# Gated linear attention: three buffers for values by chunk and states, and a step's features requested one step early

## The chip, the cores and the metric

The kernel runs on one core of a Trainium2 chip. The metric is the time of one execution on the device in microseconds (us). A plain time is the median of several timed executions; the profile is one further execution, recorded by the hardware profiler.

The core has a matmul engine (PE), a vector engine (DVE), a scalar engine (ACT), a general engine (POOL), and a queue engine (SP) that issues most DMA loads. ACT issues most stores. Each engine takes its instructions in its own order.

## The reference, cut to what matters

One layer of a hybrid token mixer on x of 2048 tokens by 1024 features: an adaptive normalisation, one projection to 13 groups of columns, three mixers (gated linear attention "GLA", a second gated linear attention "HGRN", and stick-breaking attention), gates, an output projection, a residual and a last normalisation. The stage that the change touches computes this twice, for GLA (4 heads, 64 key and 128 value features each) and for HGRN (4 heads, 64 and 64):

```python
def step(state, inp):                       # one chunk of 64 tokens
    q_c, k_c, v_c, g_c = inp
    b_cum = jnp.cumsum(g_c, axis=2)
    diff = b_cum[:, :, :, None, :] - b_cum[:, :, None, :, :]
    decay = jnp.exp(jnp.where(causal, diff, -jnp.inf))
    scores = jnp.einsum('bhtd,bhsd,bhtsd->bhts', q_c, k_c, decay)
    o_c = (jnp.einsum('bhts,bhsv->bhtv', scores, v_c)
           + jnp.einsum('bhtd,bhdv->bhtv', q_c * jnp.exp(b_cum), state))
    b_last = b_cum[:, :, -1:, :]
    state = (jnp.exp(b_last[:, :, 0, :, None]) * state
             + jnp.einsum('bhsd,bhsv->bhdv', k_c * jnp.exp(b_last - b_cum), v_c))
    return state, o_c
```

## The kernel before

The program first makes all projections and writes them to DRAM, then computes the stick-breaking attention mixed with further projections, then the linear-attention stage, and last the output stage (phase2).

The linear-attention stage has 16 steps. A step is one pair of heads and 512 tokens (8 chunks of 64): steps 0 to 7 are GLA (two pairs, four steps each), steps 8 to 15 are HGRN. In this stage PE's order is written by hand (`manual_schedule(engines={ENG.PE})`). The order on SP, ACT, DVE and POOL is made by the framework's planner when the program is built: it places an instruction by its planned readiness (inputs there, buffer free), and among ready ones by their place in the text. A tile with `bufs=2` has two buffers in turn; a new tile waits until the last reader of the tile that held its buffer is done.

A step runs as follows.

- Loads on SP: three features bc, qt, kt (128x512, 256 KB each, lines 897 to 899, three buffers each); the values once by blocks, Vn (line 823, two buffers; 512 KB in GLA, 256 KB in HGRN), and once by chunks, Vv, in two halves (line 835, two buffers; 256 KB a half in GLA, 128 KB in HGRN). Vn feeds U, Vv feeds o.
- ACT, DVE and POOL: exponentials eP (907), and of bc (910) or kt (915); products (911, 912, 916); kd (917, on POOL, written over kt in GLA and over bc in HGRN); Qd (918, three buffers).
- PE: scp (924), the scores; four transposes ptk of kd (848). ACT copies scp to S (928) and ptk to KTt (850).
- PE: 9 fill matmuls of a gate projection (269); U = KTt x Vn (858); 9 more fill matmuls; then o of the step before (880), which reads Vv, Ms, St and Qd; ACT copies it to oe (884) and stores it.
- DVE: eight state updates (867), one for each chunk, `St[n+1] = St[n] * decay + U[n]`; the last one writes the first state of the next step's tile, Sn. St has two buffers. The last step of a pair has seven updates. At the first step of a pair POOL clears the first state (831).

The order written for PE, with `i` the step:

```python
for i, tail in enumerate(gla_fast(GLA_ORDER, gp, gr_, pp, scp)):   # scp of step i
    next(tail)                  # ptk of step i
    run(fill, GLA_F[0])
    next(tail)                  # U and state updates of step i
    ...
    if i >= 8:
        with tc.issue_after(om[0].ins):
            next(ws, None)      # scale_wo: one more part of the output weights
    run(fill, GLA_F[1])
    if before is not None:
        run(before, 1)          # o of step i - 1
    before = tail
```

`om[0]` is the last state update issued; the parts of `scale_wo` (load wr, line 1019; product on POOL, 1020; wh and wl on DVE, 1023 and 1024) are placed behind it on their engines as far as it is theirs, which is DVE. The raw weights wr share two buffers (tag `wraw`) with the raw gate weights wraw (load 149, whi on ACT 150, wlo on DVE 151).

Of the kernel before, what the change touches and what calls it, by code (L numbers as in the profile page):

```python
# [8 lines left out]
F32 = mybir.dt.float32  # L9
# [3 lines left out]
AF = mybir.ActivationFunctionType  # L13
ALU = mybir.AluOpType
# [4 lines left out]
P = 128  # L19
T = 2048  # L20
# [4 lines left out]
CB = 64  # L25
GTF = 512
ORDER = (3, 2, 1, 0)
NBF = GTF // CB
# [14 lines left out]
def hybrid_mixer_kernel(ctx, tc, x, c, w_ada, b_ada, w_in, w2, bg, gnw, lbl, hnw,  # L43
                        w_out, fnw, masks, sel2, out):
    nc = tc.nc
    mm = nc.tensor.matmul
# [13 lines left out]
    class Chunks:  # L60
# [4 lines left out]
        def __getitem__(self, at):  # L65
# [4 lines left out]
    s_feat = {n: [Chunks(f"s_{n}{j}") for j in range(2)]  # L70
              for n in ("qa", "ka", "z", "qb", "fb", "da", "db", "kb")}
# [15 lines left out]
    def rms_scale(ss):  # L87
# [10 lines left out]
                            compare_op=ALU.is_gt, fill=0.0)  # L98
# [5 lines left out]
    SE = const.tile([P, 4, T // GTF, 3 * NBF], F32, name="SE")  # L104
# [119 lines left out]
    ld, ha, dv = [None], [None], [None]  # L224
# [68 lines left out]
    with tc.manual_schedule(engines={ENG.PE, ENG.DVE, ENG.Activation, ENG.Pool}):  # L293
# [132 lines left out]
        tiles = [x1, load_x(ORDER[2], p0x), None]  # L426
# [37 lines left out]
        for i in (1, 2):  # L464
            n = ORDER[i]
# [8 lines left out]
    n = ORDER[3]  # L474
# [30 lines left out]
    with tc.issue_after(ha[0].ins), tc.issue_after(dv[0].ins):  # L505
# [12 lines left out]
        loml = const.tile([P, 2], F32, name="loml")  # L518
# [10 lines left out]
    def v3(ap, t=CB):  # L529
        return ap.rearrange("p (n t) -> p n t", t=t)  # L530
# [282 lines left out]
    hpools[ORDER[2]].close()  # L813


    def load_values(pools, pr, g, GT, Sn):
        gla = pr < 2
        j = pr % 2
        dv = 128 if gla else 64
        NB = GT // CB  # L820
        vcols = (s_va if gla else s_ib)[g * GT:(g + 1) * GT, j * 2 * dv:(j + 1) * 2 * dv]
        Vn = pools.tile([P, GT // P, 2 * dv], F32, tag="Vn", name="Vn")
        nc.sync.dma_start(Vn, vcols.rearrange("(b p) d -> p b d", p=P))


        def new_s():
            return pools.tile([P, NB, dv], F32, tag="St", name="St", bufs=2)
        St = Sn
        if St is None:
            St = new_s()  # L830
            nc.gpsimd.memset(St[:, 0, :], 0.0)
        Vv = pools.tile([P, NB, dv], F32, tag="Vv", name="Vv", bufs=2)
        vr = vcols.rearrange("(n p) d -> p n d", p=CB)
        for h in range(2):
            nc.sync.dma_start(Vv[h * 64:(h + 1) * 64], vr[:, :, h * dv:(h + 1) * dv])
        return Vn, Vv, St, new_s() if g + 1 < T // GT else None
# [3 lines left out]
    def gla_tail(gr_, pp, pr, g, GT, Ms, Qd, kd, dec, Vn, Vv, St, Sn):  # L840
        gla = pr < 2
        j = pr % 2
        dv = 128 if gla else 64
        NB = GT // CB

        ptk = pp.tile([P, GT // P, P], F32, tag="ptk", name="ptk")
        for b in range(GT // P):
            nc.tensor.transpose(ptk[:, b, :], kd[:, b * P:(b + 1) * P], ident)
        KTt = gr_.tile([P, GT // P, P], F32, tag="KTt", name="KTt")
        nc.scalar.copy(KTt, ptk)  # L850
        yield


        U = [pp.tile([P, NB // 2, dv], F32, tag=f"U{e}", name=f"U{e}") for e in range(2)]
        for n in range(NB):
            rs = slice((n % 2) * 64, (n % 2) * 64 + 64)
            for h in range(2):
                mm(U[n % 2][h * 64:(h + 1) * 64, n // 2, :], KTt[rs, n // 2, h * 64:(h + 1) * 64],
                   Vn[rs, n // 2, h * dv:(h + 1) * dv], start=True, stop=True)
        for n in range(NB):  # L860
            if n + 1 < NB:
                dst = St[:, n + 1, :]
            elif Sn is not None:
                dst = Sn[:, 0, :]
            else:
                continue
            om[0] = nc.vector.scalar_tensor_tensor(dst, St[:, n, :], dec[:, n:n + 1], U[n % 2][:, n // 2, :],
                                           op0=ALU.mult, op1=ALU.add)
        yield


        no = 2 if gla else 1
        o = pp.tile([P, no, 512], F32, tag="o", name="o")[:, :, 0:GT]
        for n in range(NB):
            ns = slice(n * CB, (n + 1) * CB)
            for x, y, first in ((Vv, Ms, True), (St, Qd, False)):
                for h in range(2):
                    hs = slice(h * 64, (h + 1) * 64)
                    dst = o[:, h, ns] if gla else o[hs, 0, ns]
                    mm(dst, x[hs, n, :], y[hs, ns], start=first, stop=not first)  # L880
        for a in range(no):
            ob = 2 * j + a if gla else 4 + j
            oe = gr_.tile([P, GT], F32, tag="oe", name="oe")
            nc.scalar.copy(oe, o[:, a, :])
            nc.scalar.dma_start(s_o[ob][:, g * GT:(g + 1) * GT], oe)

    def gla_fast(pairs, gp, gr_, pp, scp):

        for pr in pairs:
            gla = pr < 2  # L890
            j = pr % 2
            s = 1.0 / 16.0 if gla else 1.0
            Sn = None
            for g in range(T // GTF):
                tsl = slice(g * GTF, (g + 1) * GTF)
                bc, qt, kt = (gp.tile([P, GTF], F32, tag=t, name=t, bufs=3) for t in ("bc", "qt", "kt"))
                nc.sync.dma_start(bc, s_feat["da" if gla else "db"][j][:, tsl])
                nc.sync.dma_start(qt, s_feat["qa" if gla else "qb"][j][:, tsl])
                nc.sync.dma_start(kt, s_feat["ka" if gla else "kb"][j][:, tsl])
                Vn, Vv, St, Sn = load_values(gr_, pr, g, GTF, Sn)  # L900

                def per_chunk(i):
                    return SE[:, pr, g, i * NBF:(i + 1) * NBF].unsqueeze(2).broadcast_to((P, NBF, CB))

                Ms, Qd = (gr_.tile([P, GTF], F32, tag=t, name=t, bufs=3) for t in ("Ms", "Qd"))
                eP = gp.tile([P, GTF], F32, tag="eP", name="eP")
                nc.scalar.activation(eP, bc, AF.Exp, scale=s)
                if gla:
                    eN, kd = bc, kt
                    nc.scalar.activation(eN, bc, AF.Exp, scale=-s)  # L910
                    nc.vector.scalar_tensor_tensor(eP, qt, 0.125, eP, op0=ALU.mult, op1=ALU.mult)
                    nc.vector.tensor_tensor(eN, kt, eN, op=ALU.mult)
                else:
                    eN, kd = kt, bc
                    nc.scalar.activation(eN, kt, AF.Exp, bias=loml[:, j:j + 1])
                    nc.vector.tensor_tensor(eP, qt, eP, op=ALU.mult)
                nc.gpsimd.tensor_tensor(v3(kd), v3(eN), per_chunk(2), op=ALU.mult)
                nc.vector.tensor_tensor(v3(Qd), v3(eP), per_chunk(0), op=ALU.mult)
                for n in range(NBF):
                    for h in range(2):  # L920
                        hs = slice(h * 64, (h + 1) * 64)
                        t0 = n * CB
                        for e in range(2):
                            mm(scp[h * 64 + 32 * e:h * 64 + 32 * e + 32, n, 32 * e:CB],
                               eN[hs, t0 + 32 * e:t0 + 32 * e + 32], eP[hs, t0 + 32 * e:t0 + CB],
                               start=True, stop=True, tile_position=(h * 64, h * 64 + 32 * e))
                S = gp.tile([P, GTF], F32, tag="S", name="S")
                nc.scalar.copy(S, scp.rearrange("p n t -> p (n t)"))
                for h in range(2):
                    hs = slice(h * 64, (h + 1) * 64)  # L930
                    nc.gpsimd.affine_select(v3(Ms[hs]), v3(S[hs]),
                                            pattern=[[0, NBF], [1, CB]], base=0,
                                            channel_multiplier=-1, compare_op=ALU.is_ge, fill=0.0)
                yield gla_tail(gr_, pp, pr, g, GTF, Ms, Qd, kd, SE[:, pr, g, NBF:2 * NBF],
                               Vn, Vv, St, Sn)

    def gla_exact(gp, pp):

# [92 lines left out]
    with ExitStack() as st:  # L1031
        gp = st.enter_context(tc.tile_pool(name="gp", bufs=2, reuse_waits="tile"))
        gr_ = st.enter_context(tc.tile_pool(name="gr", bufs=2, reuse_waits="tile"))
        pp = st.enter_context(tc.tile_pool(name="pp", bufs=1, space=PSUM))
        scp = pp.tile([P, NBF, CB], F32, name="scp")
# [17 lines left out]
        with tc.manual_schedule(engines={ENG.PE}):  # L1053
            ws = iter(())
            fill = gates()
# [202 lines left out]
    with tc.If(rv != 0):  # L1258
        with ExitStack() as st:
            act_tables("natural_log_exp_and_others")  # L1260
            gp = st.enter_context(tc.tile_pool(name="gpx", bufs=1))
            pp = st.enter_context(tc.tile_pool(name="ppx", bufs=1, space=PSUM))
# [58 lines left out]
```

## Time and profile before

| what | value |
|---|---|
| timed runs (3) | 1264.1 us median, 1262.32 to 1264.73 |
| the profiled execution | 1272.54 us, its span 1270.4 us |
| mean granted clock of PE | 0.979 |
| PE busy | 1214.5 us (96%) |
| DVE, ACT, POOL busy | 673.4 us (53%), 470.7 (37%), 155.2 (12%) |
| HBM | 113.47 MB read, 58.73 MB written |

The span runs from the first to the last instruction. A granted clock of 1.00 is PE's upper level, 2.4 GHz, 0.50 the lower, 1.2 GHz. Busy shares are means over stages with different limits.

### The profile page before, as it was taken

What the parts mean: (1) busy time and instruction counts of PE and PEld (TensorE: products, weight loads), DVE (VectorE), ACT (ScalarE), POOL (GpSimd) and SP (SyncE); (2) the same over time, 40 slices, a digit from 0 to 9 for tenths busy, and PEclk for the clock granted to TensorE, in tenths of its full rate; (3) what the DMA queues carried; (4) which work ended last, traced back from release to release, by engine and by line L of the source; (5) the groups of instructions that cost most, each with busy time, mean ns of one, the idle gap of its engine ahead of it and who ended that gap; (6) DMA issues with size and microseconds to landing.
All of it is one profiled execution on the core that took longest, in us unless ns stands there. A gap on an engine that the chain in (4) does not pass through costs nothing.

```text
span 1270.4 us, 22877 instructions
## 1 busy us (share of the span) xinstructions
PE 1214.5 (96%) x9194; PEld 993.9 (78%) x9194; DVE 673.4 (53%) x1096; ACT 470.7 (37%) x860; POOL 155.2 (12%) x193
## 2 busy tenths in 40 slices
PE   7899999999999999999999999998999897999997
PEld 7678789999989877777787766766887674777775
DVE  4865424715242272535536488865535427675652
ACT  3376422514242142322323345543333333263521
POOL 3221000002111000000000001012333303010000
PEclk8999999999999999999999999998999897999998
DMA  9765442424222511322223422138877655464521
GB/s 269 245 232 175 160 125 80 154 89 137 80 93 83 162 55 50 91 88 76 85 88 94 115 65 77 33 87 261 264 233 229 189 175 187 158 215 141 199 83 52
DMA packets 177568, 173.78 MB, mean 137 GB/s; under 512 B 39625, under 2 KB 131882, under 8 KB 177454
## 3 DMA queue, kind: packets, MB, share of 16 engines
q1 hardware_dynamic: 144970, 128.70, 33.6%
q10 hardware_dynamic: 32484, 43.54, 9.8%
q8 instruction: 74, 1.21, 0.4%
q14 instruction: 40, 0.33, 0.1%
HBM read 113.47 MB, written 58.73 MB: 136 GB/s over the span
## 4 chain that ended last, share of the span: by engine, by line
PE 70%; issue 7%; DMA 5%; DVE 5%; ACT 1%; POOL 1%; SPq 1%; ACTq 0%; POOLq 0%; DVEq 0%
PE acc L163 6%; PE acc L165 6%; PE acc L164 6%; PE av L758 6%; PE acc L269 5%; PE pt L746 4%; PE y L1196 4%; PE y L1194 4%; PE y L1195 4%; PE acc L175 4%; PE acc L177 4%; PE acc L176 4%; PE o L880 3%; PE zt L733 2%; DVE f L742 2%
## 5 line engine op out<-in xcount | busy, mean ns | idle before, releaser
L742 DVE TENSOR_TENSOR_SCAN f<-f 128x512 f32<-128x512 f32 (+3 forms) x160 | 169.7, 1090 | 29.2 <-POOL f L738 14.3
L163 PE MATMUL acc<-hTh,whi 128*128 128x512 f32 x400 | 159.0, 399 | 1.6 <-DVE stl L288 1.1
L164 PE MATMUL acc<-hTl,whi 128*128 128x512 f32 x400 | 157.1, 393 | 0.0
L165 PE MATMUL acc<-hTh,wlo 128*128 128x512 f32 x400 | 156.9, 393 | 0.0
L175 PE MATMUL acc<-whi,hTh 128*128 128x256 f32 (+1 forms) x512 | 146.3, 286 | 0.0
L177 PE MATMUL acc<-whi,hTl 128*128 128x256 f32 (+1 forms) x512 | 146.0, 285 | 0.0
L176 PE MATMUL acc<-wlo,hTh 128*128 128x256 f32 (+1 forms) x512 | 145.8, 285 | 0.0
L269 PE MATMUL acc<-hTh,whi 128*128 128x512 f32 x240 | 103.8, 433 | 1.4 <-ACT hTh L253 1.4
L1194 PE MATMUL y<-wh,hTh 128*128 128x512 f32 x256 | 102.9, 403 | 0.7 <-DVE wh L1023 0.7
L269 PE MATMUL acc<-hTl,whi 128*128 128x512 f32 x240 | 98.1, 409 | 4.1 <-DVE hTl L259 3.9
L1195 PE MATMUL y<-wl,hTh 128*128 128x512 f32 x256 | 101.8, 398 | 0.0
L1196 PE MATMUL y<-wh,hTl 128*128 128x512 f32 x256 | 100.3, 395 | 0.3 <-DVE hTl L1162 0.3
L736 ACT ACTIVATE f<-zt 128x512 f32<-128x512 f32 (+3 forms) x160 | 82.1, 537 | 48.4 <-DVE f L742 21.3
L175 PEld LDWEIGHTS acc<-whi,hTh 128*128 128x128 f32 x512 | 97.9, 191 | 0.7 <-ACT stt L202 0.4
L176 PEld LDWEIGHTS acc<-wlo,hTh 128*128 128x128 f32 x512 | 97.9, 191 | 0.3
L177 PEld LDWEIGHTS acc<-whi,hTl 128*128 128x128 f32 x512 | 97.9, 191 | 0.0
L269 PE MATMUL acc<-hTh,wlo 128*128 128x512 f32 x240 | 97.6, 407 | 0.0
L163 PEld LDWEIGHTS acc<-hTh,whi 128*128 128x128 f32 x400 | 75.2, 188 | 19.1 <-issue 2.1
L758 PE MATMUL av<-PT,V 128*64 128x128 f32 x960 | 88.8, 280 | 0.8 <-DVE PT L751 0.8
L165 PEld LDWEIGHTS acc<-hTh,wlo 128*128 128x128 f32 x400 | 75.2, 188 | 16.6 <-issue 1.4
L746 PE MATMUL pt<-ident,f 128*128 128x128 f32 x544 | 86.7, 282 | 1.0 <-DVE f L742 0.7
L164 PEld LDWEIGHTS acc<-hTl,whi 128*128 128x128 f32 x400 | 75.3, 188 | 15.1 <-issue 1.0
(206 smaller groups left out, 2094.5 us busy)
## 6 DMA issues: line engine op xcount, KB each, us to landing
wraw<-in_w_in_dram SPq DMA_DIRECT2D x36, 512.0 KB, 4.7
xt<-in_x_dram SPq DMA_DIRECT2D x16, 512.0 KB, 5.1
wa<-in_w_ada_dram SPq DMA_DIRECT2D x16, 512.0 KB, 6.0
Q<-s_qc SPq DMA_DIRECT2D x64, 128.0 KB, 3.0
ot<-s_o SPq DMA_DIRECT2D x32, 256.0 KB, 3.2
gt<-s_gate SPq DMA_DIRECT2D x32, 256.0 KB, 3.7
r<-in_x_dram SPq DMA_DIRECT2D x16, 512.0 KB, 6.2
out_dram<-r SPq DMA_DIRECT2D x15, 512.0 KB, 2.7
```

Of the source, the lines that this page charges most:

```text
L163: mm(ps, hi[:, k, :], th[:, k, :], start=(k == 0), stop=False)
L164: mm(ps, hi[:, k, :], tl[:, k, :], start=False, stop=False)
L165: mm(ps, lo[:, k, :], th[:, k, :], start=False, stop=(k == KT - 1))
L175: mm(o, th[:, k, s], hi[:, k, 0:ncols], start=(k == 0), stop=False)
L176: mm(o, th[:, k, s], lo[:, k, 0:ncols], start=False, stop=False)
L177: mm(o, tl[:, k, s], hi[:, k, 0:ncols], start=False, stop=(k == KT - 1))
L269: mm(ps, a[:, k, :], b[:, k, :], start=(k == 0 and i == 0), stop=(k == KT - 1 and i == 2))
L742: nc.vector.tensor_tensor_scan(fr, fr, fr, carry[u], op0=ALU.mult, op1=ALU.bypass)
L758: last[0] = mm(av[u * 64:(u + 1) * 64, :], (Dd if diag else V)[J][:, b, :], PT[:, b, :], start=diag, stop=(J == 0 and b == 0))
L1194: mm(y, oh[:, k, us], wh, start=(k == 0), stop=False)
L1195: mm(y, oh[:, k, us], wl, start=False, stop=False)
L1196: mm(y, ol[:, k, us], wh, start=False, stop=(k == KT - 1))
```

## The change

`load_values` takes the number of buffers for St and Vv, and `gla_fast` passes 3 in place of 2 (the fallback path `gla_exact` keeps 2). The three feature loads become a function of their own, `load_feats`. It is called for step 0 ahead of the loop, and within step i for step i + 1, ahead of the value loads of step i. Before, a step's features were loaded at its own beginning. The two nested loops become one over `steps`. The rest of the step is the same, with less indentation.

```diff
-    def load_values(pools, pr, g, GT, Sn):
+    def load_values(pools, pr, g, GT, Sn, vbufs=2):
...
-            return pools.tile([P, NB, dv], F32, tag="St", name="St", bufs=2)
+            return pools.tile([P, NB, dv], F32, tag="St", name="St", bufs=vbufs)
...
-        Vv = pools.tile([P, NB, dv], F32, tag="Vv", name="Vv", bufs=2)
+        Vv = pools.tile([P, NB, dv], F32, tag="Vv", name="Vv", bufs=vbufs)
...
-        for pr in pairs:
+        def load_feats(pr, g):
+            names = ("da", "qa", "ka") if pr < 2 else ("db", "qb", "kb")
+            tiles = [gp.tile([P, GTF], F32, tag=t, name=t, bufs=3) for t in ("bc", "qt", "kt")]
+            for t, n in zip(tiles, names):
+                nc.sync.dma_start(t, s_feat[n][pr % 2][:, g * GTF:(g + 1) * GTF])
+            return tiles
+
+
+        steps = [(pr, g) for pr in pairs for g in range(T // GTF)]
+        todo = list(steps)
+        feats = load_feats(*todo.pop(0))
+        Sn = None
+        for pr, g in steps:
...
-            Sn = None
-            for g in range(T // GTF):
-                tsl = slice(g * GTF, (g + 1) * GTF)
-                bc, qt, kt = (gp.tile([P, GTF], F32, tag=t, name=t, bufs=3) for t in ("bc", "qt", "kt"))
-                nc.sync.dma_start(bc, s_feat["da" if gla else "db"][j][:, tsl])
-                nc.sync.dma_start(qt, s_feat["qa" if gla else "qb"][j][:, tsl])
-                nc.sync.dma_start(kt, s_feat["ka" if gla else "kb"][j][:, tsl])
-                Vn, Vv, St, Sn = load_values(gr_, pr, g, GTF, Sn)
...
+            bc, qt, kt = feats
+            if todo:
+                feats = load_feats(*todo.pop(0))
+            Vn, Vv, St, Sn = load_values(gr_, pr, g, GTF, Sn if g else None, 3)
```

## Rows read from the trace of the kernel before

**Rows 1.** The page, part 1: busy us, share of the span and instructions.

```profile
PE 1214.5 (96%) x9194; PEld 993.9 (78%) x9194; DVE 673.4 (53%) x1096; ACT 470.7 (37%) x860; POOL 155.2 (12%) x193
```

**Rows 2.** Stretches: length, busy us by engine (instructions), PE's clock, DMA share, GB/s.

```profile
852.60:1034.30 181.70, 168.52 (x2885) 138.82 (x2885) 88.18 (x191) 63.33 (x109) 54.78 (x56) 0.95 0.74 225
885.63:896.36 10.73, 10.73 (x185) 9.06 (x183) 6.43 (x12) 4.62 (x8) 2.69 (x3) 1.00 0.89 290
867.91:885.63 17.72, 13.50 (x184) 11.08 (x183) 8.31 (x15) 3.98 (x7) 4.08 (x4) 0.81 0.91 287
...
960.92:969.49 8.57, 8.57 (x184) 7.04 (x183) 3.59 (x5) 2.91 (x6) 2.96 (x3) 1.00 0.78 235
969.49:979.05 9.56, 8.97 (x186) 7.26 (x182) 8.05 (x20) 3.49 (x6) 1.57 (x1) 1.00 0.79 191
979.05:992.45 13.40, 10.20 (x187) 8.07 (x183) 8.95 (x14) 5.40 (x9) 8.86 (x8) 0.87 0.83 248
1001.02:1016.40 15.38, 11.42 (x191) 9.09 (x191) 5.00 (x11) 4.22 (x7) 3.00 (x3) 0.78 0.49 144
```

**Rows 3.** Waits of PE, 852.6 to 1034.3: us in total, times, longest.

```profile
PE U L858 <- ACT KTt L850: 12.4, 5, 4.2
```

**Rows 4.** Timeline of ACT: start, us, operation, [idle before <- releaser].

```profile
863.11 0.63 ACT L907 ACTIVATE eP<-bc 128x512 f32<-128x512 f32 x1
...
871.81 0.63 ACT L907 ACTIVATE eP<-bc 128x512 f32<-128x512 f32 x1 [3.20 <-DMA bc<-s_da]
...
875.25 0.59 ACT L850 COPY KTt<-ptk 128x512 f32<-128x512 f32 x1
...
969.25 1.04 ACT L150 CAST whi<-wraw 128x1024 fp32r<-128x1024 f32 x1 [5.07 <-DMA wraw<-in_w_in_dram]
...
981.20 0.73 ACT L915 ACTIVATE kt<-kt,loml 128x512 f32<-128x512 f32 x1 [7.76 <-DMA kt<-s_kb]
...
1004.01 0.72 ACT L915 ACTIVATE kt<-kt,loml 128x512 f32<-128x512 f32 x1 [8.70 <-DMA kt<-s_kb]
```

**Rows 5.** Timeline of the SP queue: start of issue, us, what is requested.

```profile
846.17 0.34 SPq L897 DMA_DIRECT2D bc<-s_da  x1
...
853.57 0.37 SPq L823 DMA_DIRECT2D Vn<-s_va  x1
...
859.47 0.33 SPq L897 DMA_DIRECT2D bc<-s_da  x1
...
860.84 0.38 SPq L823 DMA_DIRECT2D Vn<-s_va  x1
...
862.80 0.69 SPq L897 DMA_DIRECT2D bc<-s_da  x1
...
886.88 0.60 SPq L897 DMA_DIRECT2D bc<-s_da  x1
...
963.68 0.39 SPq L149 DMA_DIRECT2D wraw<-in_w_in_dram  x1
...
976.47 0.38 SPq L1019 DMA_DIRECT2D wr<-in_w_out_dram  x1
976.94 0.42 SPq L897 DMA_DIRECT2D bc<-s_db  x1
```

**Rows 6.** Timeline of PE: U of step 0.

```profile
864.59 1.10 PE L858 MATMUL U<-Vn,KTt 64*64 64x128 f32 x32
```

**Rows 7.** Waits of DVE, 852 to 1034 us.

```profile
DVE St L867 <- PE o L880: 22.8, 8, 4.3
...
DVE Qd L918 <- PE o L880: 5.8, 2, 3.3
```

**Rows 8.** Timeline of DVE.

```profile
907.29 0.69 DVE L918 TENSOR_TENSOR Qd<-eP,SE 128x512 f32<-128x512 f32 x1 [2.52 <-PE o L880]
...
961.03 0.28 DVE L867 SCALAR_TENSOR_TENSOR St<-St,SE,U 128x64 f32<-128x64 f32 x1 [3.69 <-PE o L880]
...
962.44 1.22 DVE L1024 TENSOR_TENSOR wl<-wr,wh 128x1024 fp32r<-128x1024 f32 x1
```

More of the change, by code (lines that the diff above doesn't have):

```diff
@@ L892, in gla_fast @@
             s = 1.0 / 16.0 if gla else 1.0
-            Sn = None
-            for g in range(T // GTF):
-                tsl = slice(g * GTF, (g + 1) * GTF)
-                bc, qt, kt = (gp.tile([P, GTF], F32, tag=t, name=t, bufs=3) for t in ("bc", "qt", "kt"))
-                nc.sync.dma_start(bc, s_feat["da" if gla else "db"][j][:, tsl])
-                nc.sync.dma_start(qt, s_feat["qa" if gla else "qb"][j][:, tsl])
-                nc.sync.dma_start(kt, s_feat["ka" if gla else "kb"][j][:, tsl])
-                Vn, Vv, St, Sn = load_values(gr_, pr, g, GTF, Sn)
[L902 to L928, printed above, removed]
@@ new lines, in gla_fast, with per_chunk @@
+            bc, qt, kt = feats
+            if todo:
+                feats = load_feats(*todo.pop(0))
+            Vn, Vv, St, Sn = load_values(gr_, pr, g, GTF, Sn if g else None, 3)
+            def per_chunk(i):
+                return SE[:, pr, g, i * NBF:(i + 1) * NBF].unsqueeze(2).broadcast_to((P, NBF, CB))
+            Ms, Qd = (gr_.tile([P, GTF], F32, tag=t, name=t, bufs=3) for t in ("Ms", "Qd"))
+            eP = gp.tile([P, GTF], F32, tag="eP", name="eP")
+            nc.scalar.activation(eP, bc, AF.Exp, scale=s)
@@ new lines, in gla_fast @@
+            if gla:
+                eN, kd = bc, kt
+                nc.scalar.activation(eN, bc, AF.Exp, scale=-s)
+                nc.vector.scalar_tensor_tensor(eP, qt, 0.125, eP, op0=ALU.mult, op1=ALU.mult)
+                nc.vector.tensor_tensor(eN, kt, eN, op=ALU.mult)
+            else:
+                eN, kd = kt, bc
+                nc.scalar.activation(eN, kt, AF.Exp, bias=loml[:, j:j + 1])
+                nc.vector.tensor_tensor(eP, qt, eP, op=ALU.mult)
+            nc.gpsimd.tensor_tensor(v3(kd), v3(eN), per_chunk(2), op=ALU.mult)
@@ L929, in gla_fast @@
+            nc.vector.tensor_tensor(v3(Qd), v3(eP), per_chunk(0), op=ALU.mult)
+            for n in range(NBF):
                 for h in range(2):
                     hs = slice(h * 64, (h + 1) * 64)
[L931 to L935, printed above, removed]
+                    t0 = n * CB
+                    for e in range(2):
+                        mm(scp[h * 64 + 32 * e:h * 64 + 32 * e + 32, n, 32 * e:CB],
+                           eN[hs, t0 + 32 * e:t0 + 32 * e + 32], eP[hs, t0 + 32 * e:t0 + CB],
+                           start=True, stop=True, tile_position=(h * 64, h * 64 + 32 * e))
@@ new lines, in gla_fast @@
+            S = gp.tile([P, GTF], F32, tag="S", name="S")
+            nc.scalar.copy(S, scp.rearrange("p n t -> p (n t)"))
+            for h in range(2):
+                hs = slice(h * 64, (h + 1) * 64)
+                nc.gpsimd.affine_select(v3(Ms[hs]), v3(S[hs]),
+                                        pattern=[[0, NBF], [1, CB]], base=0,
+                                        channel_multiplier=-1, compare_op=ALU.is_ge, fill=0.0)
+            yield gla_tail(gr_, pp, pr, g, GTF, Ms, Qd, kd, SE[:, pr, g, NBF:2 * NBF],
+                           Vn, Vv, St, Sn)
```

## The prediction

> **What bounds the kernel now.** I read the page's busy shares first: TensorE (PE) works 96% of the span [rows 1], so time can only come out of the 4% in which it waits or out of work at half clock. Then the busy time by stretch. The change touches one stage, the gated-linear-attention stage, from 852.6 to 1034.3 us: 181.7 us, PE busy 168.5, granted clock 0.95 [rows 2]. Then who waited for whom on PE inside it: one cause alone, the 32 matmuls of U behind ACT's copy KTt, 12.4 us in five waits [rows 3]. PE's order is written by hand, so a wait on it is lost time.
>
> What each wait costs is read from the steps, from one step's scp matmuls to the next one's. An undisturbed GLA step takes 10.73 us and an undisturbed HGRN step 8.57 [rows 2]. Four steps are longer: A (step 1, from 867.91) 17.72, C (step 9, from 969.49) 9.56, D (step 10, from 979.05) 13.40, E (step 12, from 1001.02) 15.38. The losses are 7.0 + 1.0 + 4.8 + 6.8 = 19.6 us. They exceed the idle time because the granted clock in A, D and E is 0.81, 0.87 and 0.78 against 1.00 in a good step [rows 2]: after the wait PE works part of the step at the lower level, 1.2 GHz. 19.6 us is the most that this change can give back, if it touches nothing else.
>
> Why is KTt late? ACT takes its work in order, and the exponentials of a later step stand ahead of it. In A, eP and bc of step 2 wait for their features (eP begins at 871.81 after 3.20 us on a DMA), and KTt of step 1 runs only at 875.25. In D the exponential of kt waits 7.76 us for its load, until 981.20. In E it waits 8.70 us, until 1004.01. In C it is whi, 5.07 us on a weight load, until 969.25 [rows 4]. So late loads, and above all their place ahead of KTt on ACT, are what PE pays for.
>
> **The change part by part.** No instruction is added or removed: the same 48 feature loads, 48 value loads, exponentials and matmuls; issue on SP costs the same 0.3 to 0.6 us for each load [rows 5]. The price of the change is only in order and waits.
>
> (1) *Features one step early.* Where buffers are free, SP's order now follows the text: features 0, features 1, values 0, features 2, values 1. Before, the trace has bc of step 0 at 846.17, Vn 0 at 853.57, bc 1 at 859.47, Vn 1 at 860.84, bc 2 at 862.80 [rows 5]. Ahead of features 2 stood two sets of features and two of values; now two of features and one of values. A set of values in GLA is 512 KB and twice 256 KB, 1.05 MB; in the stretch of A the DMA engines moved 287 GB/s at a busy share of 0.91 [rows 2], so 1.05 MB is 3.7 us of saturated transfer. Features 2 land about 3.7 us earlier, KTt 1 with them, and of the 4.2 us wait [rows 3] 0.5 is left, too little, I estimate, to bring the clock down as the long ones did. I leave A 1.5 us of its 7.0: 5.5 gained, between 0 (the landing is set by something else) and 7.0.
>
> From step 3 on the move does nothing by itself. The sixth bc request, of step 5, goes out at 886.88 [rows 5], just behind the scp matmuls of step 2 (885.63, where the long step ends [rows 2]), whose end frees the one of three buffers that it takes. The requests already stand as early as their buffers allow, and those still number three.
>
> (2) *What the move pushes back.* Values 0 go behind features 1. Vn 0 would be requested near 859.5 to 861, in place of 853.57. The feature load requested at 859.47 had landed when its exponential ran at 863.11 [rows 4, 5], so within 3.6 us; Vn has twice the bytes. U of step 0 is due at 864.59 [rows 6]. I cost this at 0, its cover being the fill matmuls and scp 0 in front of U; with the cover gone it is a wait of 1 to 2 us on PE. Values 1 go behind features 2 and still have until about 871.6 (U of step 1 began as KTt 1 ended, 875.25 + 0.59 [rows 4], after 4.2 us of waiting [rows 3]). The third buffer lets Vv of step 2 go out at once, near 864 in place of 885: 0.5 MB more, 1.8 us, in the crowded stretch, but behind features 2; late next would be features 3, which nothing on PE needs before 896.36 [rows 2]. Cost 0, at most 1.8.
>
> (3) *Third buffer of Vv.* Vv waits for o of the step three back, not two. In steady state the request leaves SP at the same moment, with one step more in hand. No wait of PE names Vv [rows 3]: 0.
>
> (4) *Third buffer of St.* The last state update of a step writes the next step's St, whose buffer was read by o of the step before. DVE waited for that 22.8 us in eight steps [rows 7]. Most of it doesn't go away: next in DVE's order is Qd two steps ahead, and Qd has three buffers too, read by the same o. Where a pair ends and no such update exists, Qd pays the wait itself, 2.52 us at 907.29 [rows 8], 5.8 us in two [rows 7]. At one place it is different: from step 8 the scaled output weights wh and wl are placed behind the last state update. There the update ran at 961.03 after waiting 3.69 us, then wh, and wl at 962.44 [rows 8]. Without the wait wl ends 3.7 us earlier, and on wl hangs a chain in the shared wraw buffers: wraw requested at 963.68 [rows 5], whi at 969.25 [rows 4], then wlo, then wr, wl again and wr at 976.47, and behind that in SP's queue bc of step 13 at 976.94 [rows 5], which ACT needs before KTt 11. So C (0.6 us idle) goes: 1.0. D (3.2 us idle) goes but for 0.3: 4.5. For E the same chain, two links further, held the features of step 15; but PE itself is 5.5 us earlier by then (C and D), so the chain gains on it less. I take half of 6.8: 3.4, bounds 0 and 6.8.
>
> Sum: 5.5 + 1.0 + 4.5 + 3.4 = 14.4 us, bounds 0 and 19.6.
>
> The profiled execution took 1272.5 us, 8.4 more than the median 1264.1 of the timed runs. If all that excess lay in these waits for loads, the timed runs lose only 19.6 - 8.4 = 11.2 us, and the gain shrinks to 14.4 x 11.2 / 19.6 = 8.2. Between 8.2 and 14.4 I take the middle, 11.3: 1264.1 - 11.3 = 1252.8, rounded 1253.
>
> **What the Trainium skill says.** Its page "DMA: Bandwidth & Descriptors", section "Issuing engines are not separate DMA queues", says that all DMAs run on the same 16 engines and interleave, whoever issued them: asking earlier makes no bandwidth. By it alone, if each moved transfer only displaced another that is needed as soon, A would gain 0 and the sum be 8.9. The trace agrees as to the engines (0.91 busy in A [rows 2]), but the displaced transfer, values 1, isn't needed before 871.6, which is why I count 5.5.
>
> **The rivals.** *One place only* (chance 0.17): either the start rearranges itself and gives 0 while the wl chain gives 8.9, or the reverse, 5.5; times the same 0.58 to 1 for the profile, that is 3 to 9 us: 1255 to 1261. For it: the two parts touch different stretches. *Nothing* (0.13): requests are bound by buffers from step 3, the wait of St becomes one of Qd, and ACT's order still has the exponentials ahead of KTt, so the same loads are waited for: 1262 to 1266.5. For it speak 886.88 and 907.29; against it, that wl didn't stand behind Qd. *Slower* (0.16): ACT's order is made by a planner that believes loads quick. With features believed in hand one step earlier it puts exponentials ahead of more copies KTt, each such turn costing what A and E cost, some 7 us. It takes one turn more than those removed to end slower: with A, C, D and E kept and one turn more, at step 0 where U is due at 864.59 and features 2 land after 868, 1264 + 7 = 1271; with A gone in exchange, 1264. Against it: an ACT turn ahead of KTt 0 needs features 2 planned before scp 0, and they still stand behind 2.6 MB.
>
> **How the numbers follow.** Forecast 0.54, one place 0.17, nothing 0.13, slower 0.16. A difference under 0.2%, 2.5 us, is about what a measurement of this kernel can't tell from no change. Faster 0.71, same 0.13, slower 0.16. The likeliest case alone spans 1245 (all 19.6 us) to 1256. The 80% range goes from 1244 to 1266: it takes in one place and nothing, and leaves out most of slower.
>
> **What would show it.** Right: SP issues bc 1 before Vn 0 and Vn 0 after 859; the step from scp 1 to scp 2 is below 13 us with clock near 1.00; the last state update of step 8 runs right behind the seven before it, with wl near 959; the waits of DVE on o change line from the state update to Qd; PE's wait for KTt falls from 12.4 to below 5 us. Wrong: a wait of U in step 0 on Vn; KTt late in a step that was undisturbed; or the HGRN steps still at 13 to 15 us although wl came early, which would mean the wr chain doesn't set the features' landing.

## The result and the profile after

The kernel became slower: 1272.25 us (median of 6 runs, 1270.14 to 1275.06) against 1264.41 before (6 runs, 1262.32 to 1267.66). The ratio is 1.0069, with a 95% interval of 1.0054 to 1.0085, about 8 us. The prediction was 1253 us, faster with a chance of 0.71.

The profiled execution took 1272.16 us, as good as equal to the 1272.5 us of the one before. So the two traces seem to show no loss at all. The reason, found with a second profile of the unchanged kernel (run b_again, below), is that the execution whose rows the prediction used lost about 7 us more in this stage than the second.

The prediction counts the steps of C, D and E one short: from 0, by the scp matmuls, C is step 10, D step 11, E step 13, and A is step 1. I keep the letters. First the stage, then single steps of the kernel after, in the columns of [rows 2]: step 1 (A), step 2, step 9, C, D, E.

```profile
852.60:1034.30 181.70, 167.37 (x2890) 138.05 (x2890) 89.54 (x191) 62.77 (x109) 56.02 (x57) 0.95 0.77 226
868.65:887.10 18.45, 12.29 (x184) 10.29 (x183) 7.79 (x19) 2.94 (x6) 3.78 (x4) 0.81 1.10 279
887.10:897.83 10.73, 10.73 (x185) 9.06 (x183) 6.54 (x12) 4.62 (x8) 2.70 (x3) 1.00 0.88 294
962.05:975.65 13.60, 10.28 (x185) 8.12 (x183) 6.60 (x13) 4.33 (x7) 2.48 (x1) 0.87 0.78 211
975.65:984.24 8.59, 8.59 (x187) 7.04 (x183) 5.84 (x12) 3.31 (x6) 7.41 (x8) 1.00 0.78 233
984.24:992.81 8.57, 8.57 (x186) 7.04 (x183) 5.24 (x6) 2.67 (x6) 4.73 (x5) 1.00 0.89 260
1002.06:1016.96 14.90, 11.01 (x186) 8.72 (x182) 5.79 (x15) 4.21 (x7) 2.81 (x3) 0.77 0.56 158
```

C and D now take the length of undisturbed steps, as forecast. But A is as long as ever, E has hardly moved, and step 9, which was 8.57 us in [rows 2], is a new long step of 13.60. The same long steps of the kernel before in its second profile were A 11.74, C 9.97, D 12.27, E 15.14:

```profile
867.70:879.44 11.74, 10.87 (x183) 9.16 (x183) 8.31 (x15) 3.98 (x7) 4.08 (x4) 1.00 1.07 363
962.88:972.85 9.97, 8.95 (x186) 7.26 (x182) 8.03 (x20) 3.73 (x6) 1.88 (x1) 1.00 0.80 191
972.85:985.12 12.27, 10.18 (x186) 8.02 (x182) 9.25 (x14) 5.13 (x9) 8.96 (x8) 0.86 0.92 273
993.69:1008.83 15.14, 11.27 (x186) 8.95 (x183) 5.00 (x11) 4.22 (x7) 3.00 (x3) 0.77 0.49 147
```

Summed over the steps as length less 10.73 or 8.57 (without steps 0, 8 and 15, which take the same in every kernel or have no next scp), the first profile before loses 20.2 us, the second 12.9 and the one after 20.1. Against the second the change costs 7.2 us in this stage: 6.7 in A, 5.0 in step 9, 0.7 in step 12 and 0.1 elsewhere (0.3 in step 3, less 0.2 in step 6), less 5.1 won in C and D and 0.3 in E. That is the measured loss to within 1 us (1272.25 - 1264.41 = 7.8). Of A's 6.7 us, 5.3 are more idle time of PE (6.16 against 0.87) and 1.4 are longer busy time (12.29 against 10.87) at a granted clock of 0.81 in place of 1.00.

Who waited for whom, in the kernel after, on PE and then on DVE (total us, times, longest):

```profile
PE U L858 <- ACT KTt L850: 14.1, 5, 6.2
```

```profile
DVE Qd L926 <- PE o L880: 22.1, 9, 3.7
```

From its first step in this stage on, PE waits for KTt and nothing else. On DVE the 22.8 us of the state update have become 22.1 us of Qd [rows 7]. ACT around the two bad steps shows what stands ahead of KTt:

```profile
867.54 0.63 ACT L915 ACTIVATE eP<-bc 128x512 f32<-128x512 f32 x1 [3.45 <-DMA bc<-s_da]
868.21 0.63 ACT L918 ACTIVATE bc<-bc 128x512 f32<-128x512 f32 x1
868.76 0.60 ACT L194 ACTIVATE st<-acc 128x512 f32<-128x512 f32 x1
877.07 0.33 ACTq L195 DMA_DIRECT2D s_gate<-st  x1
877.44 0.59 ACT L936 COPY S<-scp 128x512 f32<-128x512 f32 x1 [8.08 <-DMA kt<-s_ka]
877.92 0.59 ACT L850 COPY KTt<-ptk 128x512 f32<-128x512 f32 x1
...
964.99 1.05 ACT L150 CAST whi<-wraw 128x1024 fp32r<-128x1024 f32 x1 [5.79 <-DMA wraw<-in_w_in_dram]
965.94 1.07 ACT L884 COPY oe<-o 128x512 f32<-128x512 f32 x2
...
968.48 0.58 ACT L850 COPY KTt<-ptk 128x512 f32<-128x512 f32 x1
```

In step 1, eP of step 2 did come earlier than in [rows 4], 867.54 against 871.81, as forecast (in b_again it came at 868.99, so against that execution it gained only 1.5 us). KTt of step 1 came later all the same, 877.92 against 875.25 (871.68 in b_again). Between the two stands the request of a store: a tile of the gate projection, s_gate, which ACT itself issues (L195). The 8.08 us of idle ACT before S are this wait and the issue of the store, and the profile names as releaser a load that has no data in common with it, kt of step 3. In step 9 it is whi, 5.79 us on its weights.

Why a store waits for a load can be read in the compiled program. A completion semaphore is a counter that a transfer raises when it has landed. Transfers issued by SP and by ACT take eight of them in turn, and each first waits until the previous user of its semaphore has landed; for the store, that wait is an instruction of its own on ACT, just ahead of the request. The store and its predecessor on the semaphore, in the order before and in the order after (in brackets the semaphores that each waits for; not a view of the profile):

```
before  L195 DMA s_gate1_3_138<-st_8638   [waits DMAHW0_49, Activation_49]
        L899 DMA kt_8727<-s_ka0_2_74      [waits DMAHW0_49]
after   L195 DMA s_gate1_3_138<-st_8644   [waits DMAHW3_49, Activation_49]
        L893 DMA kt_8733<-s_ka0_3_75      [waits DMAHW3_49, PE_49]
```

Before, the store waited for kt of step 2; with the features asked for a step earlier it waits for kt of step 3, requested at 867.77 and landed by about 877.07.

### The profile page after: what moved, and what is told of

It is laid out like the page before. It is cut to its first block, busy times and chain, and to the rows that moved or that the text cites. A ratio compares the mean times of both kernels' runs of the same rounds, so it can differ in the third digit from the quotient of the medians.

```text
span 1270.1 us, 22877 instructions
## 1 busy us (share of the span) xinstructions
PE 1211.8 (95%) x9194; PEld 991.1 (78%) x9194; DVE 674.3 (53%) x1096; ACT 470.5 (37%) x860; POOL 157.5 (12%) x193
```

## The experiments

The table gives the median, its ratio to the kernel before run beside it with the 95% interval, and the losses by step read from each kernel's one profile (step length less 10.73 or 8.57; "all" sums every step).

| kernel | us | ratio | 1 (A) | 2 | 9 | C + D | E | all |
|---|---|---|---|---|---|---|---|---|
| before (first profile) | 1264.41 | 1 | 7.0 | 0 | 0 | 5.8 | 6.7 | 20.2 |
| after | 1272.25 | 1.0069 [1.0054, 1.0085] | 7.7 | 0 | 5.0 | 0 | 6.3 | 20.1 |
| b_again | 1263.96 | 1.0006 [0.9986, 1.0025] | 1.0 | 0 | 0 | 5.1 | 6.6 | 12.9 |
| feat_only | 1269.37 | 1.0045 [1.0029, 1.0060] | 6.5 | 0 | 0 | 2.8 | 7.6 | 17.2 |
| bufs_only | 1269.99 | 1.0048 [1.0029, 1.0068] | 7.6 | 0 | 6.1 | 0 | 6.7 | 20.5 |
| st_only | 1266.99 | 1.0015 [1.0000, 1.0030] | 1.4 | 0 | 3.3 | 0 | 5.3 | 10.9 |
| vv_only | 1268.76 | 1.0029 [1.0015, 1.0043] | 7.5 | 0 | 0 | 3.7 | 5.5 | 18.3 |
| pool_a | 1268.73 | 1.0045 [1.0029, 1.0061] | 0 | 4.3 | 6.1 | 0 | 5.0 | 17.4 |
| one_store | 1268.56 | 1.0043 [1.0028, 1.0058] | 0 | 4.4 | 5.9 | 0 | 6.1 | 17.1 |
| pool_all_a | 1272.65 | 1.0077 [1.0048, 1.0106] | 0 | 3.9 | 4.5 | 0 | 5.7 | 14.4 |
| pool_all_b | 1266.94 | 1.0014 [0.9997, 1.0030] | 6.7 | 0 | 0 | 1.1 | 5.0 | 14.1 |
| whi_a | 1267.76 | 1.0031 [1.0017, 1.0044] | 8.4 | 0 | 0 | 1.8 | 4.3 | 15.3 |
| whi_b | 1264.11 | 0.9992 [0.9976, 1.0008] | 1.8 | 0 | 0 | 5.1 | 6.6 | 13.5 |
| pool_all_whi_a | 1263.79 | 0.9983 [0.9966, 0.9999] | 0 | 3.9 | 0 | 0.5 | 3.5 | 8.0 |
| pool_all_whi_b | 1264.84 | 0.9997 [0.9980, 1.0014] | 1.4 | 0 | 0 | 1.0 | 1.5 | 8.2 |
| best | 1259.70 | 0.9963 [0.9945, 0.9980] | 0 | 0 | 0 | 1.1 | 3.7 | 5.2 |

Three profiles lie well below the median of their own kernel: st_only's by 4.5 us, pool_all_a's by 4.2 and pool_all_whi_b's by 4.7 (there step 12 holds 4.1 of the loss); vv_only's lies 3.1 above. Their sums are read with that in mind. The time of a profile less its sum is 1249.7 to 1254.0 in all sixteen, so the steps carry most of what differs and some 4 us lie elsewhere.

**The kernel before once more, and the parts alone.** b_again is the kernel before, unedited.

> The kernel before, unchanged, for a second profile. Its first profiled execution took 1272.5 us, 8 above its own timed median of 1264.4, and showed four long steps (A 7.0, C 1.0, D 4.8, E 6.8 us lost). Theory 1 (the change exchanges one long step for others, and the first profile caught one more long step than most executions have): the time is 1262 to 1268, and a profile near 1264 shows one of A, D, E missing. Rival (recording the profile costs 8 us): the profile is again at 1272 with the same four long steps, while the timed runs stay at 1264.

Measured: no difference in time, but 11.74 us for A in place of 17.72, as theory 1 had it. ACT there:

```profile
870.30 0.33 ACTq L195 DMA_DIRECT2D s_gate<-st  x1
870.68 0.63 ACT L910 ACTIVATE bc<-bc 128x512 f32<-128x512 f32 x1 [1.06 <-DMA kt<-s_ka]
871.21 0.57 ACT L928 COPY S<-scp 128x512 f32<-128x512 f32 x1
871.68 0.59 ACT L850 COPY KTt<-ptk 128x512 f32<-128x512 f32 x1
```

The store stands ahead of KTt here too, but the load it waits for landed early enough: a wait of 1.06 us. So 6 of the 7 us that A was taken to lose aren't in this execution of the same kernel; by their median time they are not in most of the timed runs either.

feat_only keeps the early features and gives back both third buffers:

```diff
-            Vn, Vv, St, Sn = load_values(gr_, pr, g, GTF, Sn if g else None, 3)
+            Vn, Vv, St, Sn = load_values(gr_, pr, g, GTF, Sn if g else None, 2)
```

> Features one step early, St and Vv with two buffers. Theory 1: the start of the stage is that of the changed kernel (ACT's store of a gate tile waits for kt of step 3 and holds KTt of step 1, step 1 at 17 to 18.5 us), the HGRN steps are those of the kernel before (whi behind KTt of step 9, that step at 8.6 us). Time 1263 to 1268. Rival (the extra buffers alone cost the time): 1264, no difference from before.

bufs_only is the kernel before with both third buffers; st_only and vv_only have one of its two lines each:

```diff
-            return pools.tile([P, NB, dv], F32, tag="St", name="St", bufs=2)
+            return pools.tile([P, NB, dv], F32, tag="St", name="St", bufs=3 if GT == GTF else 2)
...
-        Vv = pools.tile([P, NB, dv], F32, tag="Vv", name="Vv", bufs=2)
+        Vv = pools.tile([P, NB, dv], F32, tag="Vv", name="Vv", bufs=3 if GT == GTF else 2)
```

> Three buffers for St and Vv, features requested as before. Theory 1: the HGRN steps are those of the changed kernel (wl about 3.7 us earlier, whi ahead of KTt of step 9, that step at 12 to 14 us), and step 1 is as before or 1 to 2 us longer, as Vv of step 2 moves ahead of the features of step 3. Time 1266 to 1273. Rival (the early features alone cost the time): 1264, no difference from before.

> Three buffers for St alone; Vv and the feature requests as before. Theory 2 (St's third buffer lets wl go earlier, and that puts whi ahead of KTt of step 9 on ACT): step 1 as in the kernel before (ACT's gate store waits for kt of step 2, 11 to 12 us, or 17 in some executions), step 9 at 13.5 to 14.6 us, steps 10 and 11 undisturbed; the time 1263 to 1267, as what steps 10 and 11 win (5 us) step 9 loses. Rival (St has no part in step 9): step 9 at 8.6, steps 10 and 11 as before, time 1264.

> Three buffers for Vv alone; St and the feature requests as before. Theory 2 (Vv of step 2 goes out ahead of the features of step 3, and the gate store on ACT waits for it): step 1 at 17 to 18.5 us in every execution, the HGRN steps as before (steps 10 and 11 lose 5 us, step 9 none); time 1269 to 1272. Rival (Vv's third buffer costs nothing): 1264, step 1 at 11 to 12.

Measured: the early features alone and the buffers alone each cost over 4 us, and both make A long. Not all came as expected: feat_only's time lies above its range, and bufs_only was not to make step 1 more than 2 us longer, yet it took 18.29 us; in st_only step 9 took 11.87, less than expected, and vv_only's time lies 0.2 us below its range. In the orders of before, after, feat_only and bufs_only the same store waits for four different loads; in vv_only it waits for the one of bufs_only. In feat_only, bufs_only and vv_only:

```profile
873.48 0.35 ACTq L195 DMA_DIRECT2D s_gate<-st  x1
873.87 0.58 ACT L936 COPY S<-scp 128x512 f32<-128x512 f32 x1 [5.94 <-DMA bc<-s_da]
```

```profile
873.36 0.33 ACTq L195 DMA_DIRECT2D s_gate<-st  x1
873.73 0.63 ACT L910 ACTIVATE bc<-bc 128x512 f32<-128x512 f32 x1 [5.51 <-DMA Vv<-s_va]
```

```profile
875.07 0.33 ACTq L195 DMA_DIRECT2D s_gate<-st  x1
875.45 0.63 ACT L910 ACTIVATE bc<-bc 128x512 f32<-128x512 f32 x1 [4.51 <-DMA Vv<-s_va]
```

In the programs of feat_only and bufs_only the store's predecessor on its semaphore is just that: bc of step 3 (DMAHW1) and the second half of Vv of step 2 (DMAHW2). The third buffer of Vv alone makes A long (7.5), since it lets Vv of step 2 be requested before the store. Sorted by what the store waits for, A is 11.74, 12.08, 12.48 and once 17.72 us where it is kt of step 2 (b_again, st_only, whi_b below, before), and 17.2 to 19.1 where it is a later load (after, feat_only, bufs_only, vv_only, whi_a below). The third buffer of St alone leaves A as it was and moves the loss of C and D to step 9; its time is at the edge of no change.

**Moving the stores off ACT.** pool_a is the kernel after with all gate stores issued by POOL; one_store moves only one of them, the one of A:

```diff
-    def ev_act(*acts):
+    def ev_act(*acts, q=nc.scalar):
...
-                nc.scalar.dma_start(dst[:, n * 512:(n + 1) * 512], st)
+                q.dma_start(dst[:, n * 512:(n + 1) * 512], st)
...
-                    ev_act((s_gate[j], AF.Copy, 1.0))(ps, n)
+                    ev_act((s_gate[j], AF.Copy, 1.0), q=nc.gpsimd if (j, n) == (1, 3) else nc.scalar)(ps, n)
```

(pool_a has `q=nc.gpsimd` in the last line.)

> The changed kernel with the gate stores of this stage's fill issued by POOL in place of ACT, so that ACT has no store ahead of KTt of step 1 that must wait for a load. Theory 1: step 1 falls from 18.4 us to 11 to 13, the time by 5 to 7 us, to 1265 to 1268. Rival (KTt of step 1 waits for the features themselves, through the exponentials ahead of it): step 1 stays at 17 to 18 us, the time at 1272.

> The changed kernel with one single store moved, that of the gate tile which ACT issues in step 1 (second gate block, chunk 3): POOL issues it. Theory 2 (this one instruction, waiting for kt of step 3, holds KTt of step 1): step 1 at 10.7 to 11.5 us; as later stores keep their waits, step 2 may lose up to 4.5; step 9 as in the changed kernel; time 1266 to 1270. Rival (several stores or the loads themselves): step 1 stays at 17 us or more, time 1272.

Measured: pool_a's step 1 is undisturbed, its time 0.7 us above the range. one_store came as expected: with that single store moved, step 1 is undisturbed and step 2 becomes long. The two steps of one_store, then its ACT:

```profile
868.00:878.72 10.72, 10.72 (x183) 9.06 (x182) 6.51 (x17) 3.00 (x5) 4.48 (x5) 1.00 1.14 281
878.72:893.88 15.16, 12.28 (x184) 10.27 (x183) 6.53 (x12) 4.61 (x8) 2.69 (x3) 0.89 1.08 317
```

```profile
869.72 0.59 ACT L850 COPY KTt<-ptk 128x512 f32<-128x512 f32 x1
...
882.62 1.01 ACTq L885 DMA_DIRECT2D s_o<-oe  x2
883.72 0.58 ACT L936 COPY S<-scp 128x512 f32<-128x512 f32 x1 [3.81 <-DMA gb<-s_gr]
884.20 0.63 ACT L915 ACTIVATE eP<-bc 128x512 f32<-128x512 f32 x1
884.73 0.58 ACT L850 COPY KTt<-ptk 128x512 f32<-128x512 f32 x1
```

KTt of step 1 comes at 869.72 in place of 877.92, 8.2 us earlier, of which 0.6 is that the step itself begins earlier. This shows that the store's place on ACT is what made A of this kernel long. The loss of step 2 has the same face: the store of oe (L885) ahead of KTt, held until gb has landed. Moving all of ACT's stores should then free both:

```diff
-            nc.scalar.dma_start(s_o[ob][:, g * GT:(g + 1) * GT], oe)
+            nc.gpsimd.dma_start(s_o[ob][:, g * GT:(g + 1) * GT], oe)
```

pool_all_a is pool_a with this line, pool_all_b the kernel before with both.

> The changed kernel with all stores of the linear-attention stage (gate tiles and oe) issued by POOL, so that no store stands in ACT's order there. Theory 2 (ACT's stores wait for the completion of the transfer eight places earlier in the common order of transfers, and the change moves a late load into that place): steps 1 and 2 fall to 10.7 to 11.5 us; step 9 stays at 13.5 to 14.6 us (whi ahead of KTt); time 1263 to 1267. Rival (the loads themselves come too late for the exponentials ahead of KTt, since the values of step 2 now compete with them): steps 1 or 2 still lose 4 us or more, time 1268 to 1272.

> The kernel before with all stores of the linear-attention stage issued by POOL. Theory 2: step 1 at 10.7 to 11.5 us (1.0 us at most gained on an ordinary execution), the HGRN steps lose 10 to 12 us as before; time 1261 to 1265, and the changed kernel in the same form is slower only by step 9, 0 to 4 us. Rival: the difference between the two forms stays at 7 to 8 us.

Both missed. pool_all_a took 1272.65 us, and its step 2 still loses 3.9: with no store on ACT, eP of step 4 waits 3.02 us for its bc, with KTt behind it. SP and ACT of pool_all_a:

```profile
876.59 1.53 SPq L893 DMA_DIRECT2D bc<-s_da  x1
```

```profile
883.34 0.63 ACT L915 ACTIVATE eP<-bc 128x512 f32<-128x512 f32 x1 [3.02 <-DMA bc<-s_da]
883.88 0.57 ACT L850 COPY KTt<-ptk 128x512 f32<-128x512 f32 x1
```

In pool_all_b it is eP of step 2 that waits 4.94 us in A. So the stores weren't the only thing late: loads come late too. In pool_all_a bc of step 4 leaves SP only at 876.59, behind both halves of Vv of step 2 among others; with Vv back at two buffers (best against pool_all_whi_a, below) it leaves 4.1 us earlier, and step 2 loses nothing. The page "DMA: Bandwidth & Descriptors" of the Trainium skill, section "Issuing engines are not separate DMA queues", says that all transfers run on the same 16 engines, whoever starts them. No run here measures that sharing by itself; what fits it is that moving the stores to POOL freed ACT and left the loads late. That pool_all_a's median is that of the kernel after, with a smaller sum in its profile, I can't explain; the profile is the fastest of six runs that go up to 1278.40.

**whi off ACT.** whi_a and whi_b let DVE make the high half of the gate weights, in the kernel after and before:

```diff
-    def split_w(col0, pool, ncols, step, bufs=None, low=nc.vector):
+    def split_w(col0, pool, ncols, step, bufs=None, low=nc.vector, high=None):
...
-            nc.scalar.copy(hi[:, :, s:s + step], raw)
+            if high is None:
+                nc.scalar.copy(hi[:, :, s:s + step], raw)
+            else:
+                high.tensor_copy(hi[:, :, s:s + step], raw)
...
-                w = split_w(gate_cols[j], wp, P, P)
+                w = split_w(gate_cols[j], wp, P, P, high=nc.vector)
```

> The changed kernel with the high part whi of this stage's gate weights copied by DVE in place of ACT. Theory 2 (in step 9 KTt waits on ACT behind whi, which waits for its weights): step 9 falls from 13.6 to 8.6 to 9.5 us, step 1 stays at 18 us; time 1265 to 1269. Rival (KTt of step 9 waits for the features of step 11): step 9 stays at 13 to 14 us, time 1271 to 1274.

> The kernel before with whi copied by DVE in place of ACT. Theory 2: steps 10 and 11 lose 2 us in place of 5, step 13 4 in place of 6.5, step 1 as before; time 1258 to 1262, and the changed kernel in the same form (1267.8) is 6 to 8 us slower, by step 1. Rival (whi matters only in the changed kernel): 1264.

In whi_a step 9 is undisturbed and the time 1.0031 of before in place of 1.0069: 5.0 us lost there in the profile, about 4.8 given back in time. whi_b missed: C and D lose the same 5.1 us as in b_again, since D, the longer one, waited for the exponential of kt and not for whi [rows 4]. In whi_b's trace ACT waits for kt ahead of both copies KTt, 6.20 us in C and 7.28 in D.

**Both, and a version that beats both kernels.** pool_all_whi_a and pool_all_whi_b have all three edits, in the kernel after and before. best is pool_all_whi_a with Vv back at two buffers:

```diff
-        Vv = pools.tile([P, NB, dv], F32, tag="Vv", name="Vv", bufs=vbufs)
+        Vv = pools.tile([P, NB, dv], F32, tag="Vv", name="Vv", bufs=2)
```

> The changed kernel with both: all stores of the stage on POOL, whi on DVE. Theory 2: steps 1, 2 and 9 at their undisturbed lengths, the steps 10 to 13 lose 6 to 8 us, time 1257 to 1262, faster than the kernel before. Rival: 1268 to 1272.

> Features one step early, three buffers for St, two for Vv, all stores of the stage on POOL, whi on DVE. Theory 2: with 0.5 MB less in the crowded start the features of step 4 are requested some 3 us earlier, step 2 loses 0 to 2 us in place of 3.9, step 1 none, step 13 3 to 4; time 1257 to 1261, faster than both kernels. Rival (something other than the extra Vv holds back the features of step 4): step 2 stays at 14.6 us, time 1264.

> The kernel before with all stores of the stage on POOL and whi on DVE: the control of the fastest form (features early, three St, 1259.7). Theory 2 (without ACT's other waits the early features and the third St buffer are worth what the forecast said, step 1 and steps 10, 11): step 1 at 15 to 17.5 us, as features 2 land behind values 1, steps 10 and 11 lose 2 to 5; time 1264 to 1267, 5 us or more above the fastest form. Rival (the two relocations are the whole gain of the fastest form): 1258 to 1261.

pool_all_whi_a missed: 1263.79 us, with step 2 as long as in pool_all_a. best came as expected and is faster than either kernel, 1259.70 us. Its steps 1 and 2 are undisturbed, and bc of step 4 goes out at 872.40 in place of 876.47 in pool_all_whi_a. Its waits of PE, then SP, then step 1:

```profile
PE U L861 <- ACT KTt L853: 2.7, 2, 1.8
```

```profile
872.40 0.49 SPq L896 DMA_DIRECT2D bc<-s_da  x1
```

```profile
867.22:877.94 10.72, 10.72 (x183) 9.06 (x182) 6.34 (x17) 3.01 (x5) 3.76 (x5) 1.00 1.10 332
```

pool_all_whi_b is its control (its time as expected, its step 1 at 12.11 us below): the moved instructions without the change are worth nothing (0.9997), so by the two ratios the early features and St's third buffer bring 0.34%, some 4 us, once ACT's stores and whi are out of the way. Vv's third buffer takes 0.20% away there (0.9983 against 0.9963); the two intervals overlap, so this last figure isn't clear of the noise, though step 2 points the same way, 14.67 us with it and 10.72 without.

## Why the prediction was wrong

**The base.** The execution that was costed is of the same kernel, but A in it took 6 us more than in b_again. The prediction scaled its gains by 0.57 (11.2 / 19.6; where it writes 0.58, that is a slip) to 1 for the excess of 8.4 us; it spread over four steps what lay nearly all in one. Of the 19.6 us that it called "the most that this change can give back" the timed runs had about 12.7 in these four steps, if b_again's profile stands for them.

**Part (1), A: the step that failed.** "Features 2 land about 3.7 us earlier, KTt 1 with them." The first half held against the trace that was costed: eP of step 2 began 4.3 us earlier. The second didn't, since bc wasn't the last thing ahead of KTt. Already in the trace of before a store stood between them, issued at 873.88 after waiting for kt of step 2, with 1.80 us of idle ACT behind it; the prediction read past it:

```profile
873.88 0.33 ACTq L195 DMA_DIRECT2D s_gate<-st  x1
874.25 0.63 ACT L910 ACTIVATE bc<-bc 128x512 f32<-128x512 f32 x1 [1.80 <-DMA kt<-s_ka]
```

Asking for features earlier put more loads in front of that store, and it now waits for one of step 3. In place of 5.5 us won, A is 6.7 us longer than in b_again (18.45 against 11.74).

**Part (2).** SP's order came as forecast, Vn of step 0 behind the second bc (857.40 and 854.23, 2 us or more earlier than the prediction had Vn), and U of step 0 did not wait. That "late next would be features 3, which nothing on PE needs before 896.36" was false: by way of the store KTt of step 1 needed them. What was costed here at 0 is the other side of A's loss.

**Part (3), Vv: 0.** Wrong: alone it costs 0.29%, in A. "No wait of PE names Vv" is true of before, but the buffer lets 0.5 MB be requested into the crowded steps 1 and 2. The prediction saw this transfer and put it at 1.8 us at most.

**Part (4), St.** The mechanism was right to its details: the last state update of step 8 runs with the seven others, wl at 959.44 (forecast: near 959), wraw at 960.70 in place of 963.68, C and D free. In DVE and SP of the kernel after:

```profile
956.24 2.56 DVE L867 SCALAR_TENSOR_TENSOR St<-St,SE,U 128x64 f32<-128x64 f32 x8 [0.96 <-PE U L858]
...
959.44 1.23 DVE L1032 TENSOR_TENSOR wl<-wr,wh 128x1024 fp32r<-128x1024 f32 x1
```

```profile
960.70 0.38 SPq L149 DMA_DIRECT2D wraw<-in_w_in_dram  x1
```

What it missed is the next lateness. In the new order whi stands ahead of KTt of step 9 and waits for that weight load until 964.99, so KTt runs at 968.48. The 5.1 us won in C and D are paid in step 9, the prediction's own sign of being wrong: "KTt late in a step that was undisturbed". E was put at 3.4; it brought 0.3.

**The rivals.** "Slower" is what came, in part by one turn on ACT ahead of a KTt, in step 9, where I had sought it at step 0. In A it was a store, not an exponential, that stood ahead, and its place had not turned; the load that it waits for had changed. feat_only and vv_only lose with step 9 undisturbed, by A.

**What stays open.** The losses by step are read from one profile of each kernel, and A of the kernel before shows that one profile may mislead by 6 us. That the store waits for the earlier user of its semaphore rests on the programs and on four orders in which the named load changes with it; its number was not changed by itself. Why A varies between executions of one kernel, and what sets E, which lost 1.5 to 7.6 us in these kernels, was not tested.

## What to carry to other kernels

Before costing an earlier load, list everything that stands on the in-order engine ahead of the critical instruction, the requests of stores included, and ask of each what releases it after the change. Compare the profiled execution with the median first, and with a second profile of the same kernel if they differ by as much as the gain. Another buffer is also another transfer in flight at a crowded place: add it where the freed order is seen, not everywhere at once.

## What the hardware showed unexpectedly

A store of one 128x512 tile held ACT idle for 8.08 us, its own issue included, until an unrelated load had landed, in the trace of the kernel after. A load of 128x512 requested at 867.77 landed only about 9.3 us later, in a step whose DMA share is 1.10, where one requested at 859.47 in [rows 5] had landed within 3.6 us. One kernel's step 1 took 17.72 us in one execution, with a granted clock of 0.81, and 11.74 in another, with 1.00.
